# Experts' rows of blocks 13 to 16 added to the residual block by block, the read-back and the per-layer projection moved

## The chip, the core and the metric

The kernel runs on one core of a Trainium2 chip. TensorE (PE) multiplies, with its weight loads shown apart (PEld); VectorE (DVE), ScalarE (ACT) and GpSimd (POOL) do the elementwise work; SyncE (SP) issues the DMAs of the weights. The metric is the device time of one execution in microseconds, the median of several runs. One further execution was taken with the hardware profiler, and all rows below are from it.

## What is computed

Two models' layers run one after the other on 512 tokens of width 1024; everything is float32. The change touches the end of the second block: a mixture of experts (32 experts in four groups, one group and two experts of it for each token) and, behind it, a gated per-layer term.

```
y = 0
for grp in range(4):
    hid = silu(hf @ w_gate[e]) * (hf @ w_up[e])        # experts of width 256
    y = y + (hid * combine) @ w_down[e]                # two experts for each token
x = x + y
ple = rms_norm(p @ w_ple, ple_norm_g)
x = x + sigmoid(rms_norm(x, ple_gate_norm_g) @ w_ple_gate) * ple
```

## The kernel before

The residual is kept on the chip as eight tiles `h[k]` of 128 columns of the width by 512 tokens. The experts run in 17 blocks (NPOS) of 128 rows, two experts of 64 rows each; block 16 holds rows that didn't fit, and its experts' numbers are read from a register. For a block, the rows are gathered from DRAM (`xd`) by an indirect DMA on POOL's queue, turned by eight transposes on TensorE (`turn_rows`), multiplied with gate and up weights in two halves (`up_products`, `expert_up`), turned (`expert_turn`) and multiplied with the down weights (`expert_down`). The loop in `experts` lets block i's up products run with block i-1's turn and down products.

The weights come through `Ring`: 102 loads of 1 MB, four `w_eg` and two `w_ed` for a block, all issued by SP in the order in which they are used. A buffer is refilled with the next load when its matmuls are done (`release`, `fill`). There are 15 buffers that are refilled (eight `rawa`, three `rawb`, three `raw`, one `rawc`) and four pairs that serve once. `ring.gone` names the buffers that are no longer refilled (`rawb` and `rawc`, from block 8 on), `ring.hold` takes the next released buffers out for other uses (three at block 9, for `w_ple` and the projection's result; four at block 16). So eight buffers are left from block 9 on.

The results of blocks 0 to 13 (below NST = 14) are scattered to `yd` in DRAM by an indirect DMA on POOL's queue, each token's two rows to two places. Those of blocks 14 to 16 stay on the chip, split into a high and a low part (`pair_rows`), with a matrix of ones and zeros that spreads rows to tokens (`spread`). At block 16 four ring buffers are taken and `yd` is read back into them, four DMAs of 1 MB. Behind the last block and a branch (`overflow`, not taken here), `combine` multiplies the three blocks' parts by their spreads into eight PSUM banks (48 matmuls), adds the two halves of each read-back tile on VectorE and adds them to the same banks by 32 products with the identity. `per_layer` then adds the banks to the residual one by one, splits it (`ph`, `pl`), multiplies with `w_pg` in three-term products, and gates.

The projection `p @ w_ple` (`ple_steps`, 48 matmuls) runs in the middle of blocks 12 and 13 (PLE = 11). Its norm's row factors are formed in `per_layer`, where POOL multiplies the eight tiles by them.

All instructions of an engine run in the order in which the scheduler put them; a DMA that waits for its buffer holds up the DMAs behind it in SP's order. The lines that the steps name:

```
ring.gone = [self.merged] + [b for b in self.early if any(b[0] is x for x in self.spare)]   # 1691, block PLE - 3
ring.hold += 3                                                                              # 1693, block PLE - 2
ring.hold += TT                                                                             # 1707, block NPOS - 1
nc.sync.dma_start(y[tt], yd.rearrange("(a t p) d -> t p a d", a=2, t=TT)[tt])               # 1722
```

Of the kernel before, what the change touches and what calls it, by code (L numbers as in the profile page):

```python
# [22 lines left out]
P = 128  # L23
T = 512
# [28 lines left out]
NEX = 2 * (1 + OB)  # L53
NST = 14

# [334 lines left out]
class Kernel:  # L390
# [5 lines left out]
    ROWS = 7  # L396
    PLE = 11
    F0 = 6
# [1234 lines left out]
    def experts(self, rp, halves, *logits):  # L1633
# [4 lines left out]
        with ExitStack() as ctx:  # L1638
# [7 lines left out]
            tp = turns.enter_context(self.pool("eturn", side="right"))  # L1646
            xe, hid, turned, pairs, begun = {}, {}, {}, [], []
            gath = [tp.tile([P, D], F32, name=f"gath{i}") for i in range(2)]
# [23 lines left out]
            with ExitStack() as c2:  # L1672
# [5 lines left out]
                def turn():  # L1678
                    turned[i - 1] = self.expert_turn(tp, hid.pop(i - 1))
                    if between is not None:  # L1680
                        run(between)
                fetch(2)
                ple = own = None
                for i in range(NPOS + 1):
                    if i == 2:
                        next(routing)
                    if i == 5:
                        r["blocks"] = nc.values_load(r["over"][0:1, 0:1], min_val=0, max_val=NEX - 1,
                                                     skip_runtime_bounds_check_because=self.WHY)
                    if i == self.PLE - 3:  # L1690
                        ring.gone = [self.merged] + [b for b in self.early if any(b[0] is x for x in self.spare)]
# [12 lines left out]
                    if i == self.PLE + 1:  # L1704
                        next(ple)
                    if i == NPOS - 1:
                        ring.hold += TT
                    if i < NPOS:
                        between = rows(i + 1) if 0 < i < NPOS - 1 else None
                        act = self.expert_up(begun if i == 0 else self.up_products(xe.pop(i), ring), table[:, :, i], turn if i else None)  # L1710
                        if 0 < i < NPOS - 2:
                            fetch(i + 2)
                    else:
                        between = None
                        turn()
                    if i in (self.PLE + 1, self.PLE + 2):
                        next(ple)
                    if i == NPOS - 1:
                        y, taken = [], [ring.take() for _ in range(TT)]
                        for tt in range(TT):  # L1720
                            y.append(taken[tt].rearrange("p (a d) -> p a d", a=2))
                            nc.sync.dma_start(y[tt], yd.rearrange("(a t p) d -> t p a d", a=2, t=TT)[tt])
                    if i > 0:
                        acc = [self.bank() for _ in range(2)]
                        self.expert_down(turned.pop(i - 1), acc, ring)
                        if i - 1 >= NST:
                            ys = [late.tile([P, D], FR, name=f"ys{n}{i - 1}") if i < NPOS else tp.tile([P, D], FR, name=f"ys{n}", tag=f"xe{n}")
                                  for n in range(2)]
# [10 lines left out]
                downed = self.downed  # L1739
                self.overflow(tp, r)  # L1740
                sums = self.combine(pairs, y, downed)
            turns.close()
        return sums, ple, taken[0]

# [13 lines left out]

    def combine(self, pairs, y, downed):

        nc = self.nc
        o = [self.bank() for _ in range(KD)]
        for k in range(KD):
            for i, ((hi, lo), spread) in enumerate(pairs):
                for x in (hi, lo):
                    nc.tensor.matmul(o[k], x[:, P * k:P * k + P], spread, start=i == 0 and x is hi, stop=False)  # L1766
        for tt in range(TT):
            z = y[tt][:, 0]
            with self.tc.issue_after(downed.ins):
                nc.vector.tensor_tensor(z, z, y[tt][:, 1], op=ALU.add)  # L1770
            for k in range(KD):
                nc.tensor.matmul(o[k][:, P * tt:P * tt + P], z[:, P * k:P * k + P], self.ident, start=False, stop=tt == TT - 1)  # L1772
        return o

# [278 lines left out]
    def expert_up(self, steps, scales, between=None):  # L2053
# [6 lines left out]
        self.hidden = self.act(a, o[:, 0:256], AF.Silu, scale=scales[:, 0:1])  # L2060
        nc.vector.scalar_tensor_tensor(a, a, scales[:, 1:2], o[:, 256:512], op0=ALU.mult, op1=ALU.mult)
        return a
# [68 lines left out]
    def ple_steps(self, halves, late, room):  # L2131
# [16 lines left out]
        for m in range(KD):  # L2148
# [15 lines left out]
            if m % 4 == 3:  # L2164
                yield

    def per_layer(self, sums, ple, room):

        nc, W = self.nc, self.W
        with ExitStack() as ctx:  # L2170
# [14 lines left out]
            def gated(m, rb, o, ts):  # L2185
# [3 lines left out]
                nc.vector.scalar_tensor_tensor(x, x, 1.0, y, op0=ALU.add, op1=ALU.mult)  # L2189
                nc.vector.scalar_tensor_tensor(x, x, 0.5, self.h[m][:, ts], op0=ALU.mult, op1=ALU.add)  # L2190
# [16 lines left out]
            ps = self.bank()  # L2207
            for i, x in enumerate((self.ssq, self.ple_ssq)):
                for tt in range(TT):
                    nc.tensor.matmul(ps[:, TT * i + tt:TT * i + tt + 1], x[:, tt * P:tt * P + P], self.ones[:, 0:1], start=True, stop=True)  # L2210
            r = self.stat.tile([P, 2 * TT], F32, name="rcols", tag="rcol2")
            nc.vector.tensor_scalar(r, ps[:, :2 * TT], 1.0 / D, EPS, ALU.mult, ALU.add)
            nc.vector.reciprocal(r, r)
            self.act(r, r, AF.Sqrt)
            rows = []
            for i in range(2):
                product(3 + i)
                rows.append(self.to_rows(r[:, TT * i:TT * i + TT], ("rbc", "ssq")[i]))
            for x in self.ple:
                nc.gpsimd.tensor_tensor(x, x, rows[1], op=ALU.mult)  # L2220
            for m in range(KD - 1):
                if m > 4:
                    product(m)
                gated(m, rows[0], bank[m], slice(0, T))
            hi, lo = W.next("w_pg")
            for hf in range(2):
                ts = slice(256 * hf, 256 * hf + 256)
                o = self.bank()[:, 0:256]
                self.mm3(o, [((hi[:, P * k:P * k + P], lo[:, P * k:P * k + P]), (xs[k][0][:, ts], xs[k][1][:, ts])) for k in range(KD)])
                gated(KD - 1, rows[0], o, ts)  # L2230

# [14 lines left out]
```

## Time and profile before

| | us |
|---|---|
| median of three runs (2161.9, 2162.22, 2170.76) | 2162.22 |
| profiled execution, its own time | 2171.21 |
| span of the profile, first to last instruction | 2169.5 |
| TensorE busy | 2093.6 |
| VectorE busy | 1065.2 |
| ScalarE busy | 790.3 |
| POOL busy | 303.4 |

TensorE is busy in 97% of the span, but a busy TensorE includes matmuls that overlap and are modelled, and the share is a mean over stages with different limits. The share of the DMA engines, slice by slice, is low through most of the kernel and near full from about 1844 us on, where the experts' weights are streamed. The experts run from about 1828 to 2084 us, and from there to 2169.5 us come the combining, the gate's products and the output.

### The profile page before, as it was taken

To read this page: it belongs to the slowest core of one execution; us is meant where nothing else is said; L and a number is where in the kernel's file an instruction comes from. 1 tells how busy PE (TensorE), PEld (TensorE's weight loads), DVE (VectorE), ACT (ScalarE), POOL (GpSimd) and SP (SyncE) were. 2 spreads that over 40 slices of the span, in tenths; PEclk is the share of its full clock that TensorE was granted. 3 is DMA by queue.
4 is the path that set the end of the run, shared out by engine and by line. 5 is a ranking of instruction groups with operands and counts; after the bars stand their busy time and mean duration, and the time that the engine had idled before them with its cause. 6 is when DMAs were issued, how large, how long until landed. Compare 5 with 4: busy or idle time off the path is not lost. (4 is left out here: it accounts for less than half of the span.)

```text
span 2169.5 us, 25893 instructions
## 1 busy us (share of the span) xinstructions
PE 2093.6 (97%) x10282; PEld 1629.8 (75%) x10282; DVE 1065.2 (49%) x1928; ACT 790.3 (36%) x1189; POOL 303.4 (14%) x394
## 2 busy tenths in 40 slices
PE   8999999999999999999999999999999996998987
PEld 6678788888889878888788888888888884333456
DVE  7888644344467563554544344435654433112146
ACT  5676432223357443333433223342453221111223
POOL 3312200000013021221200000020110111111203
PEclk9899999999999999999999999999999998999999
DMA  5123332222224310101022222232211285999961
GB/s 188 59 79 109 150 111 98 99 88 95 88 72 147 115 35 15 40 24 55 21 96 97 90 95 97 88 136 78 79 58 67 96 323 198 374 420 416 380 278 39
DMA packets 71251, 281.72 MB, mean 130 GB/s; under 512 B 8859, under 2 KB 14235, under 8 KB 58452
## 3 DMA queue, kind: packets, MB, share of 16 engines
q1 hardware_dynamic: 60388, 264.63, 33.2%
q0 software_dynamic: 5504, 12.30, 1.5%
q10 hardware_dynamic: 5232, 3.07, 0.5%
q8 instruction: 83, 1.36, 0.2%
q14 instruction: 44, 0.36, 0.1%
HBM read 272.40 MB, written 15.73 MB: 133 GB/s over the span
## 5 line engine op out<-in xcount | busy, mean ns | idle before, releaser
L274 ACT ACTIVATE whi<-raw 128x1024 fp32r<-128x1024 f32 (+2 forms) x249 | 261.9, 1054 | 629.8 <-PE bank L421 578.6
L421 PE MATMUL bank<-xh,whi 128*128 128x512 f32 x1160 | 462.4, 399 | 8.6 <-ACT xh L431 7.8
L421 PE MATMUL bank<-xh,wlo 128*128 128x512 f32 x1160 | 456.4, 394 | 0.0
L421 PE MATMUL bank<-xl,whi 128*128 128x512 f32 x1160 | 453.1, 391 | 0.0
L275 DVE TENSOR_TENSOR wlo<-raw,whi 128x1024 fp32r<-128x1024 f32 (+2 forms) x249 | 314.8, 1268 | 213.9 <-ACT whi L274 210.0
L421 PEld LDWEIGHTS bank<-xh,whi 128*128 128x128 f32 x1160 | 219.3, 189 | 54.9 <-ACT xh L431 7.8
L421 PEld LDWEIGHTS bank<-xh,wlo 128*128 128x128 f32 x1160 | 218.4, 188 | 50.7 <-DVE wlo L275 0.3
L421 PEld LDWEIGHTS bank<-xl,whi 128*128 128x128 f32 x1160 | 219.0, 189 | 49.6 <-issue 1.2
L448 POOL TENSOR_TENSOR ssq<-ssq,sq 128x512 f32<-128x512 f32 x27 | 40.2, 1489 | 793.2 <-ACT sq L435 793.2
L421 PE MATMUL bank<-hidh,whi 128*128 128x512 f32 x352 | 137.0, 389 | 0.0
L421 PE MATMUL bank<-hidh,wlo 128*128 128x512 f32 x352 | 137.0, 389 | 0.0
L421 PE MATMUL bank<-hidl,whi 128*128 128x512 f32 x352 | 136.9, 389 | 0.0
L2049 PE MATMUL bank<-rawa,xe 128*64 128x512 f32 x328 | 93.8, 628 | 9.9 <-DMA rawa<-w_eg 6.3
L435 ACT ACTIVATE prob<-bank 128x512 f32<-128x512 f32 (+1 forms) x96 | 57.2, 596 | 110.8 <-PE bank L1238 81.3
L822 DVE TENSOR_TENSOR fb<-bank,rows 128x512 f32<-128x512 f32 x44 | 30.4, 690 | 133.5 <-PE bank L421 133.5
L1221 PEld LDWEIGHTS acc<-v,prob 128*128 128x128 f32 x640 | 79.8, 192 | 6.2 <-POOL prob L1248 2.3
L1221 PE MATMUL acc<-v,prob 128*128 128x96 f32 x640 | 82.2, 274 | 1.4 <-POOL prob L1248 1.4
L421 PEld LDWEIGHTS bank<-hidh,wlo 128*128 128x128 f32 x352 | 66.1, 188 | 13.9
L421 PEld LDWEIGHTS bank<-hidl,whi 128*128 128x128 f32 x352 | 66.1, 188 | 13.8
L421 PEld LDWEIGHTS bank<-hidh,whi 128*128 128x128 f32 x352 | 66.1, 188 | 13.6
L819 DVE TENSOR_TENSOR fa<-bank,rows 128x512 f32<-128x512 f32 x44 | 30.4, 690 | 88.2 <-PE bank L421 88.2
L2049 PEld LDWEIGHTS bank<-rawa,xe 128*64 128x64 f32 x328 | 27.4, 144 | 59.2 <-issue 48.5
(562 smaller groups left out, 3696.2 us busy)
## 6 DMA issues: line engine op xcount, KB each, us to landing
raw<-w_gu SPq DMA_DIRECT2D x44, 1024.0 KB, 4.8
rawa<-w_eg SPq DMA_DIRECT2D x41, 1024.0 KB, 14.1
raw<-w_dn SPq DMA_DIRECT2D x20, 1024.0 KB, 4.8
raw<-w_eg SPq DMA_DIRECT2D x16, 1024.0 KB, 13.7
rawa<-w_ed SPq DMA_DIRECT2D x16, 1024.0 KB, 14.9
raw<-w_mix SPq DMA_DIRECT2D x12, 1024.0 KB, 4.9
raw<-w_ed SPq DMA_DIRECT2D x10, 1024.0 KB, 15.7
rawb<-w_eg SPq DMA_DIRECT2D x7, 1024.0 KB, 17.1
```

The source lines that it names most:

```text
L274: nc.scalar.activation(hi, r, AF.Copy)
L275: nc.vector.tensor_tensor(lo, r, hi.bitcast(F32), op=ALU.subtract)
L421: i = nc.tensor.matmul(o, a, b, start=first and n == 0, stop=last and n == N - 1)
L435: return self.nc.scalar.activation(o, i, f, **kw)
L448: self.nc.gpsimd.tensor_tensor(self.ssq, self.ssq, sq, op=ALU.add)
L819: nc.vector.tensor_tensor(a, og, rbc, op=ALU.mult)
L822: nc.vector.tensor_tensor(b, ov, rbc, op=ALU.mult)
L1221: i = nc.tensor.matmul(a[:, h * AW:h * AW + AW], e[:K, h * P:h * P + P], v, start=first and h == 0, stop=last and h == HPG - 1)
L2049: last = nc.tensor.matmul(o[s], xe[:, 4 * pi + k, s], w(k), start=pi == 0 and k == 0, stop=pi == 1 and k == 3)
```

## The change

NST goes from 14 to 13, so block 13 stays on the chip too. The parts of blocks 13, 14 and 15 are no longer kept for `combine`: `add_block` multiplies one block's part by its spread, bank by bank, and VectorE adds each bank to `h[k]` at once, in the middle of the next block (or behind `expert_down` for block 15). Only block 16 is left to `combine`, 16 matmuls. The read-back is taken at the end of block 14, into buffers held from block 13 on; `add_rows` adds its halves on POOL, transposes the tiles on TensorE and adds the banks to `h[k]`, within block 16. `ring.gone` is set at block 0. PLE goes from 11 to 6: the projection runs in blocks 7 and 8, three buffers are held at block 4, and the norm's factors and POOL's eight multiplications follow in block 9. In `per_layer` the row statistics of the projection and POOL's multiplications are gone, and the factor 0.5 has moved into the norm's factors.

```diff
-NST = 14
+NST = 13
-    PLE = 11
+    PLE = 6
...
+                    while adds:
+                        run(adds.pop(0))
...
-                    if i == self.PLE - 3:
+                    if i == 0:
                         ring.gone = [self.merged] + [b for b in self.early if any(b[0] is x for x in self.spare)]
...
+                    if i == NST:
+                        ring.hold += TT
                     if i == NPOS - 1:
-                        ring.hold += TT
+                        adds.append(self.add_rows(y))
...
-                    if i in (self.PLE + 1, self.PLE + 2):
+                    if i in (self.PLE + 1, self.PLE + 2, self.PLE + 3):
                         next(ple)
-                    if i == NPOS - 1:
-                        y, taken = [], [ring.take() for _ in range(TT)]
-                        for tt in range(TT):
-                            y.append(taken[tt].rearrange("p (a d) -> p a d", a=2))
-                            nc.sync.dma_start(y[tt], yd.rearrange("(a t p) d -> t p a d", a=2, t=TT)[tt])
...
-                            pairs.append((self.pair_rows(*ys, acc), self.spread(late.tile([P, T], FR, name=f"spread{i - 1}"), r, i - 1)))
+                            ys = [late.tile([P, D], FR, name=f"ys{n}", bufs=2) for n in range(2)]
+                            part = self.pair_rows(*ys, acc), self.spread(late.tile([P, T], FR, name="spread", bufs=2), r, i - 1)
+                            if i < NPOS:
+                                adds.append(self.add_block(*part))
...
+                    if i == NST + 1:
+
+                        y = [ring.take() for _ in range(TT)]
+                        for tt in range(TT):
+                            nc.sync.dma_start(y[tt].rearrange("p (a d) -> p a d", a=2), yd.rearrange("(a t p) d -> t p a d", a=2, t=TT)[tt])
...
+    def block_sum(self, part, spread, k):
+
+        o = self.bank()
+        for x in part:
+            self.nc.tensor.matmul(o, x[:, P * k:P * k + P], spread, start=x is part[0], stop=x is part[1])
+        return o
+
+    def add_block(self, part, spread):
+        for k in range(KD):
+            o = self.block_sum(part, spread, k)
+            self.nc.vector.tensor_tensor(self.h[k], self.h[k], o, op=ALU.add)
+            yield
+
+    def add_rows(self, y):
+
+        for x in y:
+            self.nc.gpsimd.tensor_tensor(x[:, :D], x[:, :D], x[:, D:], op=ALU.add)
+        for k in range(KD):
+            o = self.bank()
+            for tt, x in enumerate(y):
+                self.nc.tensor.transpose(o[:, P * tt:P * tt + P], x[:, P * k:P * k + P], self.ident)
+            self.nc.vector.tensor_tensor(self.h[k], self.h[k], o, op=ALU.add)
+            yield
+
+    def combine(self, part, spread):
+        return [self.block_sum(part, spread, k) for k in range(KD)]
...
+        r = self.rms_cols(ssq, tag="rcol2")
+        nc.vector.tensor_scalar(r, r, 0.5, None, ALU.mult)
+        rows = self.to_rows(r)
+        for x in self.ple:
+            nc.gpsimd.tensor_tensor(x, x, rows, op=ALU.mult)
+        yield
...
-            for x in self.ple:
-                nc.gpsimd.tensor_tensor(x, x, rows[1], op=ALU.mult)
```

How the change moves instructions is shown at three places. The first is SP's order in the first blocks, the refills of the ring behind block 1's and 2's matmuls (a row is the issuing line, the buffer, the source and the shape). Before:

```order
L343 DMA rawa7_13935<-w_ed 128x2048
L343 DMA rawb0_13925<-w_ed 128x2048
L343 DMA rawb1_13926<-w_eg 128x2048
L343 DMA rawb2_13927<-w_eg 128x2048
L343 DMA raw_14211<-w_eg 128x2048
L343 DMA raw_14212<-w_eg 128x2048
L343 DMA raw_14213<-w_ed 128x2048
L343 DMA rawc_14325<-w_ed 128x2048
L343 DMA rawa0_13928<-w_eg 128x2048
```

and now:

```order
L343 DMA rawa7_13935<-w_ed 128x2048
L343 DMA raw_14211<-w_ed 128x2048
L343 DMA raw_14212<-w_eg 128x2048
L343 DMA raw_14213<-w_eg 128x2048
L343 DMA rawa0_13928<-w_eg 128x2048
L343 DMA rawa1_13929<-w_eg 128x2048
L343 DMA rawa2_13930<-w_ed 128x2048
L252 DMA rawa3_13931<-w_ple 128x2x1024
L343 DMA rawa6_13934<-w_ed 128x2048
```

The refills of `rawb` and `rawc` are gone, and the load of `w_ple` into `rawa3` stands here.

The second is SP's order at the last expert weights. Before, the loads of `w_ed` for blocks 15 and 16 (the rows ISA set the address of an expert read from a register), the first two reads of `yd`, and the branch:

```order
L343 DMA rawa6_13934<-w_ed 128x2048
L343 DMA rawa7_13935<-w_ed 128x2048
L343 ISA
L343 DMA raw_14211<-w_ed 128x2048
L343 ISA
L343 DMA raw_14212<-w_ed 128x2048
L1722 DMA raw_14213<-yd_104 128x2x1024
L1722 DMA rawa0_13928<-yd_104 128x2x1024
L1688 TENSOR_LOAD over_14346
L2109 COMPARE_AND_BRANCH
```

and now, from the four `w_eg` of block 15 on (the two `w_ed` are block 14's, the register load belongs to block 16):

```order
L343 DMA rawa2_13930<-w_eg 128x2048
L343 DMA rawa6_13934<-w_eg 128x2048
L343 DMA rawa7_13935<-w_eg 128x2048
L343 DMA raw_14211<-w_eg 128x2048
L1744 DMA raw_14212<-yd_104 128x2x1024
L1744 DMA raw_14213<-yd_104 128x2x1024
L1744 DMA rawa0_13928<-yd_104 128x2x1024
L1744 DMA rawa1_13929<-yd_104 128x2x1024
L343 DMA rawa2_13930<-w_ed 128x2048
L343 DMA rawa6_13934<-w_ed 128x2048
L612 TENSOR_LOAD over_14346
L343 ISA
```

The four reads of `yd` have moved from behind the last `w_ed` to a place ahead of the last ten expert weights: two `w_ed` of block 14, and then the four `w_eg` of block 16, two `w_ed` of block 15 and two of block 16, which follow.

The third is VectorE's order behind the branch, the start of the tail. Before, three of the four adds of read-back halves, splits of `w_pg` (`wlo`), and the first residual tile:

```order
L2109 UNCONDITIONAL_BRANCH
L1770 TENSOR_TENSOR rawa0_13928<-rawa0_13928 128x1024
L1770 TENSOR_TENSOR rawa1_13929<-rawa1_13929 128x1024
L1770 TENSOR_TENSOR rawa2_13930<-rawa2_13930 128x1024
L275 TENSOR_TENSOR wlo_16655<-rawa6_13934,whi_16654 128x1024
L275 TENSOR_TENSOR wlo_16659<-rawa6_13934,whi_16658 128x1024
L2196 TENSOR_TENSOR h0_76<-h0_76,bank_16554 128x512
L275 TENSOR_TENSOR wlo_16663<-rawa7_13935,whi_16662 128x1024
L275 TENSOR_TENSOR wlo_16667<-rawa7_13935,whi_16666 128x1024
L432 SCALAR_TENSOR_TENSOR pl0_16680<-h0_76,vecs_86,ph0_16679 128x512
L2196 TENSOR_TENSOR h1_77<-h1_77,bank_16555 128x512
```

and now:

```order
L2126 UNCONDITIONAL_BRANCH
L2219 TENSOR_TENSOR h0_76<-h0_76,bank_16734 128x512
L275 TENSOR_TENSOR wlo_16767<-rawa7_13935,whi_16766 128x1024
L275 TENSOR_TENSOR wlo_16771<-rawa7_13935,whi_16770 128x1024
L275 TENSOR_TENSOR wlo_16775<-raw_14211,whi_16774 128x1024
L275 TENSOR_TENSOR wlo_16779<-raw_14211,whi_16778 128x1024
L432 SCALAR_TENSOR_TENSOR pl0_16792<-h0_76,vecs_86,ph0_16791 128x512
L2219 TENSOR_TENSOR h1_77<-h1_77,bank_16737 128x512
```

The adds of read-back halves are gone from here, and four splits of `w_pg` instead of two stand between the first add to the residual and its low part `pl0`.

On TensorE, the 16 matmuls of `add_block` stand in the first half of the next block (ten ahead of the rest of that half, six behind it) for blocks 13 and 14, and behind `expert_down` of block 15 for that block. The 32 transposes of `add_rows` stand ahead of block 16's second half.

## Rows read from the trace of the kernel before

**Rows 1.** Busy time by stretch: PE, PEld, DVE, ACT, POOL, clock, DMA share, GB/s

```profile
1860.00:2000.00 140.00, 129.56 (x611) 49.66 (x610) 24.63 (x50) 24.12 (x46) 20.51 (x21) 1.00 1.01 416
2020.00:2040.00 20.00, 20.00 (x85) 8.95 (x85) 1.78 (x4) 6.76 (x12) 7.13 (x6) 1.00 0.92 351
2040.00:2080.00 40.00, 36.50 (x158) 12.45 (x158) 5.70 (x10) 5.78 (x12) 1.00 (x1) 1.00 1.01 410
```

**Rows 2.** Timeline, VectorE, the gated products that end blocks 6, 7, 12, 13

```profile
1917.84 0.48 DVE L2061 SCALAR_TENSOR_TENSOR eact<-eact,etable,bank 128x256 f32<-128x256 f32 x1 [3.28 <-ACT eact L435]
...
1929.53 0.48 DVE L2061 SCALAR_TENSOR_TENSOR eact<-eact,etable,bank 128x256 f32<-128x256 f32 x1 [3.27 <-ACT eact L435]
...
2013.30 0.48 DVE L2061 SCALAR_TENSOR_TENSOR eact<-eact,etable,bank 128x256 f32<-128x256 f32 x1 [12.37 <-ACT eact L435]
...
2033.29 0.48 DVE L2061 SCALAR_TENSOR_TENSOR eact<-eact,etable,bank 128x256 f32<-128x256 f32 x1 [12.38 <-ACT eact L435]
```

**Rows 3.** Timeline of TensorE around the last block and the combining matmuls

```profile
2065.38 0.64 PE L2049 MATMUL bank<-rawa,xe 128*64 128x512 f32 x1 [0.95 <-DMA rawa<-w_eg]
...
2070.34 3.22 PE L2049 MATMUL bank<-rawa,xe 128*64 128x512 f32 x13 [1.30 <-DMA rawa<-w_eg]
...
2079.62 4.36 PE L2082 MATMUL bank<-raw,eh 128*64 128x512 f32 x16 [0.53 <-ACT eh L435]
2086.67 12.88 PE L1766 MATMUL bank<-spread,ys 128*128 128x512 f32 x48 [2.70 <-DVEq L2109]
```

**Rows 4.** Timeline of all engines in the tail (start, length, engine, line, operation)

```profile
2105.17 0.69 DVE L2196 TENSOR_TENSOR h<-h,bank 128x512 f32<-128x512 f32 x1 [4.81 <-PE bank L1772]
2105.78 2.35 DVE L275 TENSOR_TENSOR wlo<-rawa,whi 128x1024 fp32r<-128x1024 f32 x2
2108.05 0.74 DVE L432 SCALAR_TENSOR_TENSOR pl<-h,vecs,ph 128x512 fp32r<-128x512 f32 x1
...
2128.01 1.03 PE L2210 MATMUL bank<-ones,plessq 128*128 128x1 f32 x8
...
2142.64 12.77 POOL L2220 TENSOR_TENSOR rawa<-rawa,rows 128x512 f32<-128x512 f32 x8 [17.37 <-ACT rows L435]
...
2158.23 0.28 PE L421 MATMUL bank<-ph,wlo 128*128 128x256 f32 x1
...
2164.91 0.42 DVE L2187 TENSOR_TENSOR raw<-bank,rows 128x256 f32<-128x256 f32 x1
```

**Rows 5.** DMA queues from 1700 to 2100 us: packets, MB, share of time

```profile
q1 hardware_dynamic: 18827, 120.72, 75.3%
q0 software_dynamic: 4464, 8.11, 5.6%
```

**Rows 6.** Timeline of SP: refills of the ring in blocks 0 to 4

```profile
1835.57 0.33 SPq L343 DMA_DIRECT2D rawa<-w_eg  x1
...
1860.61 5.39 SPq L343 DMA_DIRECT2D rawb<-w_eg  x2
1866.10 4.73 SPq L343 DMA_DIRECT2D raw<-w_eg  x2
...
1873.93 0.33 SPq L343 DMA_DIRECT2D rawc<-w_ed  x1
...
1894.31 0.38 SPq L343 DMA_DIRECT2D rawa<-w_eg  x1
```

**Rows 7.** Timeline of SP: the read-back's issues

```profile
2068.22 0.38 SPq L1722 DMA_DIRECT2D raw<-yd  x1
2069.06 17.39 SPq L1722 DMA_DIRECT2D rawa<-yd  x3
```

**Rows 8.** Timeline of TensorE behind the routing's gather, block 0

```profile
1828.06 1.94 PE L2035 MATMUL bank<-ident,gath 128*128 128x128 f32 x8 [6.00 <-DMA gath<-xd,gidx]
1829.93 5.61 PE L2049 MATMUL bank<-rawa,xe 128*64 128x512 f32 x16
...
1837.28 1.07 PE L2035 MATMUL bank<-ident,gath 128*128 128x128 f32 x8
```

More of the change, by code (lines that the diff above doesn't have):

```diff
@@ L1646, in experts @@
             tp = turns.enter_context(self.pool("eturn", side="right"))
-            xe, hid, turned, pairs, begun = {}, {}, {}, [], []
+            xe, hid, turned, begun, adds = {}, {}, {}, [], []
             gath = [tp.tile([P, D], F32, name=f"gath{i}") for i in range(2)]
@@ L1714, in experts @@
                         between = None
+                        while adds:
+                            run(adds.pop(0))
                         turn()
-                    if i in (self.PLE + 1, self.PLE + 2):
+                    if i in (self.PLE + 1, self.PLE + 2, self.PLE + 3):
                         next(ple)
-                    if i == NPOS - 1:
-                        y, taken = [], [ring.take() for _ in range(TT)]
-                        for tt in range(TT):
-                            y.append(taken[tt].rearrange("p (a d) -> p a d", a=2))
-                            nc.sync.dma_start(y[tt], yd.rearrange("(a t p) d -> t p a d", a=2, t=TT)[tt])
                     if i > 0:
@@ L1737, in experts @@
                         hid[i] = act
+                    if i == NST + 1:
+                        y = [ring.take() for _ in range(TT)]
+                        for tt in range(TT):
+                            nc.sync.dma_start(y[tt].rearrange("p (a d) -> p a d", a=2), yd.rearrange("(a t p) d -> t p a d", a=2, t=TT)[tt])
                 assert W.ld == len(W.order)
-                downed = self.downed
                 self.overflow(tp, r)
-                sums = self.combine(pairs, y, downed)
+                sums = self.combine(*part)
             turns.close()
-        return sums, ple, taken[0]
+        return sums, y[0]
     def spread(self, out, r, blk):
@@ L1757, in pair_rows @@
         return hi, lo
-    def combine(self, pairs, y, downed):
-        nc = self.nc
-        o = [self.bank() for _ in range(KD)]
-        for k in range(KD):
[L1764 to L1773, printed above, removed]
+    def block_sum(self, part, spread, k):
[4 more added lines that the diff above has]
+    def add_block(self, part, spread):
+        for k in range(KD):
+            o = self.block_sum(part, spread, k)
[12 more added lines that the diff above has]
+        return [self.block_sum(part, spread, k) for k in range(KD)]
     def router(self, kp, steps):
@@ L2060, in expert_up @@
         self.hidden = self.act(a, o[:, 0:256], AF.Silu, scale=scales[:, 0:1])
[L2061 removed]
+        self.scaled = nc.vector.scalar_tensor_tensor(a, a, scales[:, 1:2], o[:, 256:512], op0=ALU.mult, op1=ALU.mult)
         return a
@@ L2165, in ple_steps, with per_layer @@
                 yield
-    def per_layer(self, sums, ple, room):
+        r = self.rms_cols(ssq, tag="rcol2")
[4 more added lines that the diff above has]
+        yield
+    def per_layer(self, sums, room):
         nc, W = self.nc, self.W
@@ L2189, in gated @@
                 nc.vector.scalar_tensor_tensor(x, x, 1.0, y, op0=ALU.add, op1=ALU.mult)
-                nc.vector.scalar_tensor_tensor(x, x, 0.5, self.h[m][:, ts], op0=ALU.mult, op1=ALU.add)
+                nc.vector.tensor_tensor(x, x, self.h[m][:, ts], op=ALU.add)
                 nc.sync.dma_start(self.out[m * P:m * P + P, ts], x)
@@ L2206, in per_layer @@
                         terms(m, early[m], k - lag, k - lag + 1)
[L2207 to L2218, printed above, removed]
-            for x in self.ple:
-                nc.gpsimd.tensor_tensor(x, x, rows[1], op=ALU.mult)
+            r = self.rms_cols(self.ssq, tag="rcol2")
+            product(3)
+            rows = self.to_rows(r)
+            product(4)
             for m in range(KD - 1):
@@ L2223, in per_layer @@
                     product(m)
-                gated(m, rows[0], bank[m], slice(0, T))
+                gated(m, rows, bank[m], slice(0, T))
             hi, lo = W.next("w_pg")
@@ L2229, in per_layer @@
                 self.mm3(o, [((hi[:, P * k:P * k + P], lo[:, P * k:P * k + P]), (xs[k][0][:, ts], xs[k][1][:, ts])) for k in range(KD)])
-                gated(KD - 1, rows[0], o, ts)
+                gated(KD - 1, rows, o, ts)
 def kernel(**inputs):
```

2 lines of the change are left out of this document (removed).

## The prediction

> **What bounds the kernel now.** I read the busy time by stretches first. From 1860 to 2080 us, where most of the 17 expert blocks run, the DMA share is 1.01 at 410 to 416 GB/s, except around 2020 to 2040 (0.92) [rows 1]. The reader should see that TensorE is also busy there, and ask which of the two ends the waits. The block ends say it: blocks 6 and 7 are 11.7 us apart, as long as their matmuls take, while the two blocks that also carry the per-layer projection end 20.0 us apart [rows 2]. In the last two blocks the matmuls wait for weights again (0.95 and 1.30 us), and the two pairs of loads of block 16 arrive 4.96 us apart [rows 3]. So the DMA queue bounds the end of the experts, and what counts is how many megabytes stand ahead of the last w_ed, and whether the queue ever runs empty.
>
> Behind the experts stands a tail in which the queue no longer counts. The last expert matmul ends at 2083.98, 48 matmuls of `combine` take 12.88 us [rows 3], 32 products with the identity follow, and the first add to the residual starts only at 2105.17. The last matmul of all starts at 2158.23, the span ends at 2169.5, 11.1 us after it: VectorE is late, because eight multiplications on POOL (12.77 us) run until 2155.4 and it needs their results [rows 4].
>
> **Unit prices.** The SP queue moved 120.72 MB in 75.3% of 400 us [rows 5]: 115 loads of 1 MB in 301 us, 2.62 us each in a full queue. The 31 gathers and scatters of rows (17 and 14 by the loops) took 5.6% of the same stretch, 0.72 us each. Six loads, a gather and a scatter per block make 17.2 us of queue against 11.7 us of matmuls. Half an `expert_up`, or an `expert_down`, is 3.2 to 3.5 us [rows 3].
>
> **Fewer buffers from the start.** The order of SP shows that rawb and rawc are no longer refilled after their first use and that three rawa are held at block 4 (they were at block 9). Before, 23 refills were issued from 1835.57 to the one at 1894.31, three rawb, three raw and one rawc among them [rows 6]. Now it is 16, w_ple included, the last of them behind the same block's matmuls, by the order of SP. Blocks 0 to 4 run on loads that came earlier, so TensorE's pace doesn't change, and the queue has 16 x 2.62 + 6 x 0.72 = 46 us of work in 59 us: empty for 13 us. Before it was empty for 1.6 us in the projection's stretch (0.92 of 20 us) [rows 1]; moved to blocks 7 and 8 the projection finds a queue that lags, so that gap goes. Net +11.5 us (bounds 0, if the queue weren't the bound later, to 13). The projection itself costs as much TensorE time at blocks 7 and 8 and is covered by the queue. Its eight POOL multiplications, 12.8 us at block 9, stand ahead of the scatter of block 8 and the gather for block 13, which is used in block 12; I price them at nothing, the cover being the 5.5 us by which the queue exceeds the matmuls in each of blocks 10 to 12. One scatter less: -0.7 us.
>
> **The read-back ahead of ten loads.** The change's words put it behind all weights; SP's order doesn't. The four reads of `yd` stand behind block 15's w_eg and ahead of w_ed of 14, w_eg of 16, w_ed of 15 and w_ed of 16. Before, they were the last but for w_pg: two issued at 2068 to 2069, the others behind the branch [rows 7]. In a full queue they cost 4 x 2.62 = 10.5 us, waited for by `expert_down` of block 14, with all of TensorE's order behind it.
>
> **Four buffers and more matmuls.** From block 13 on four buffers are left, two pairs A and B that take turns. Let X be the landing of block 15's last w_eg. Before: six loads (15.7 us) and a half block (3.5): block 16's second half ends at X + 19.2, measured 2073.98, so X is 2054.8. Now: read-back X + 10.5, w_ed of 14 at X + 15.7, down(14) ends X + 19.3 and frees A for the second w_eg pair of 16. The first pair lands at X + 20.9, TensorE goes on with a matmul, a turn (0.4), ten matmuls of block 14's rows at 12.88 / 48 = 0.27 (2.7), the rest of the half (3.0): X + 27.0; six more (1.6): X + 28.6; `add_rows`. Its 32 transposes are 4.3 us by the gather's eight in 1.07 [rows 8] or 5.5 us if VectorE's eight adds at 0.69 [rows 4] pace them; the order has them wait for VectorE's banks, so 5.0. POOL's four adds of 1024 columns, 2.6 to 3.3 us each by the eight of 512 in 12.77 [rows 4], end by X + 16, under the wait. Second half: X + 37.1. Against X + 19.2 that is 17.9 us, 10.5 of them the read-back and 7.4 the rest (bounds 3, all additions hidden under the wait, to 14, none of them).
>
> From there to the last expert matmul it was 10.0 us [rows 3]; now down(15) 3.5, sixteen matmuls of block 15's rows 4.3, turn and eviction 1.1, down(16) 3.6: 12.5 us, +2.5. TensorE will stand still about 8 us ahead of down(14). After the 6.00 us wait in the routing, eight transposes took 1.94 instead of 1.07 and 16 matmuls 5.61 instead of 3.22 to 3.65 us [rows 8]: down(14) loses some 2.5 us, of which 1.2 get past the landing at X + 20.9. [...]
>
> Last expert matmul: 11.5 - 0.7 + 17.9 + 2.5 + 1.2 = 32.4 us later.
>
> **The tail.** Before, from the start of `combine` (C, 2086.67) to the end: 82.8 us. Now 16 matmuls instead of 48 and 32 products. The first residual add starts at C + 1 instead of C + 18.5; behind it stand four w_pg splits at 1.2 us instead of two (rows 4 has two in 2.35), since the loads come only now, so the first `pl` ends at C + 7.1 instead of C + 22.1: 15.0 us won. Eight small matmuls of row statistics less: 1.0 us (a row's 1.03). With POOL's multiplications gone, VectorE keeps up and the end follows the last matmul by 4.9 instead of 11.1 us (4.6 from the last gate's start at 2164.91 to the end, 0.3 for the matmul's own end) [rows 4]: 6.2 us. Together 22.2 us (18 to 27).
>
> **Sum.** +32.4 - 22.2 = +10.2 us. The profiled execution's own time is 2171.21 us, 9 us above the median of the runs (2162.22); I add to the median: 2172.4 us, +0.47%.
>
> **Rivals.** *The queue has slack.* If the matmuls, not the queue, set the pace in blocks 10 to 14, neither the empty 13 us nor the read-back costs anything; of the added 13.6 us of matmuls ahead of block 16's second half 7.5 hide under its former waits, +6.1 + 2.5 - 22.2 = -13.6 us: 2148.6. It decides where the DMA share in these blocks falls under 1. For it: the 0.92 of the projection's stretch; against it: 17.2 us of queue against 11.7, and 1.01 on either side of it [rows 1].
>
> *Only one of the two delays reaches the end.* The early gap is made up, or the read-back runs behind the weights after all as the words say: one term of 10.5 to 11.5 goes, about -1 us: 2161. For it: blocks 7 and 8 take 20 us for 17.2 us of queue. Against it: an empty queue's time isn't made up unless it would have been empty later too.
>
> [...]
>
> **How the numbers follow.** Forecast 0.54 (2164 to 2180), one delay only 0.19, clock 0.15, slack 0.12. A measurement here can tell some 0.5% (10.8 us: 2151.4 to 2173.0) from no change. Faster by more: the slack case, 0.12. Within: the one-delay case and half the forecast, 0.47. Slower by more: the rest, 0.41. The range from 2154 to 2185 leaves out the slack case and the far end of the clock's.
>
> **What would show it.** In the profile after: DMA share under 1 between 1865 and 1900; reads of yd issued ahead of ten weight loads; a wait of about 8 us of down(14) for w_ed; last expert matmul near 2116; `combine` to end near 60 us. The forecast is wrong if that matmul ends before 2106, or if the share falls under 1 in blocks 10 to 14.

## The result

The changed kernel takes 2175.36 us, median of 12 runs, against 2163.76 us for the kernel before in the same series; the ratio of the runs is 1.0051, with a 95% interval from 1.0039 to 1.0063. It is slower by half a per cent, 11.0 us by that ratio. The medians are 11.6 us apart, and one run of the kernel before, at 3477.43 us, is far off all others. The forecast was 2172.4 us and +10.2 us, so sign and size held. The terms behind it held less well: two errors of some 5 us each, which ran against each other, lie among them, and the experiments below say which.

### The profile page after: what moved, and what is told of

It is laid out like the page before. It is cut to its first block, busy times and chain, and to the rows that moved or that the text cites. A ratio compares the mean times of both kernels' runs of the same rounds, so it can differ in the third digit from the quotient of the medians.

```text
span 2170.0 us, 25913 instructions
## 1 busy us (share of the span) xinstructions
PE 2089.4 (96%) x10266; PEld 1626.3 (75%) x10266; DVE 1075.3 (50%) x1965; ACT 792.9 (37%) x1192; POOL 308.6 (14%) x397
## 5 line engine op out<-in xcount | busy, mean ns | idle before, releaser
L2066 PE MATMUL bank<-rawa,xe 128*64 128x512 f32 x352 | 106.1, 617 | 10.8 <-DMA rawa<-w_eg 7.1
## 6 DMA issues: line engine op xcount, KB each, us to landing
rawa<-w_ed SPq DMA_DIRECT2D x21, 1024.0 KB, 10.6
```

The source lines that it names most:

```text
L2066: last = nc.tensor.matmul(o[s], xe[:, 4 * pi + k, s], w(k), start=pi == 0 and k == 0, stop=pi == 1 and k == 3)
```

## The profile after

The profiled execution of the changed kernel took 2171.69 us with a span of 2170.0 us, only 0.5 us more than that of the kernel before. The two can't be laid on each other as they are, because the execution of before lost time ahead of all that was changed. Two rows of TensorE show where: the 16 matmuls of block 1's first half (start, length, engine, line, operation, the idle time before). Before:

```profile
1845.59 6.31 PE L2049 MATMUL bank<-rawa,xe 128*64 128x512 f32 x16 [3.65 <-issue]
```

and after:

```profile
1840.50 3.65 PE L2066 MATMUL bank<-rawa,xe 128*64 128x512 f32 x16 [3.66 <-issue]
```

The same matmuls behind the same wait took 6.31 us in one execution (granted clock 0.57) and 3.65 in the other (1.00). With 5.1 us from stages ahead of it, the execution of before ends block 2 at 1871.06, that after at 1863.30. So all comparisons below start at block 2's end, read from VectorE's gated product that ends a block, and go in two pieces: to the gated product of block 16 (the last up products), and from there to the span's end. Before, these rows are

```profile
1871.06 0.48 DVE L2061 SCALAR_TENSOR_TENSOR eact<-eact,etable,bank 128x256 f32<-128x256 f32 x1 [3.28 <-ACT eact L435]
...
2074.53 0.48 DVE L2061 SCALAR_TENSOR_TENSOR eact<-eact,etable,bank 128x256 f32<-128x256 f32 x1 [9.11 <-ACT eact L435]
```

and after

```profile
1863.30 0.48 DVE L2078 SCALAR_TENSOR_TENSOR eact<-eact,etable,bank 128x256 f32<-128x256 f32 x1 [2.40 <-ACT eact L435]
...
2092.83 0.48 DVE L2078 SCALAR_TENSOR_TENSOR eact<-eact,etable,bank 128x256 f32<-128x256 f32 x1 [1.11 <-ACT eact L435]
```

That is 203.47 us before and 229.53 us after, 26.1 us more for the experts. From block 16's product to the end of the span (2169.5 and 2170.0) it is 94.97 and 77.17 us, 17.8 us less. The sum is +8.3 us, a little under the 11.0 us of the runs.

**The early queue**, as [rows 1] show it for later stretches: the 60 us that begin 27.3 us ahead of block 2's end (busy time of PE, PEld, DVE, ACT, POOL, then the granted clock, the DMA share and GB/s). Before and after:

```profile
1843.80:1903.80 60.00, 58.21 (x284) 23.24 (x286) 11.05 (x25) 8.60 (x17) 9.09 (x9) 0.94 0.93 378
```

```profile
1836.00:1896.00 60.00, 56.34 (x288) 22.55 (x286) 17.74 (x46) 10.96 (x20) 9.53 (x9) 1.00 0.86 330
```

At 416 GB/s the queue would move 25.0 MB here. After, it moved 19.8 and so was 12.4 us short. Before, it moved 22.7 and was already 5.5 us short. The difference is 6.9 us, but the two clocks differ (0.94 and 1.00): with its slow matmuls inside, the stretch of before starts 2.7 us of work later. Two of the kernels below have the same clock here, e9, which refills as before, and e11, which refills as after:

```profile
1836.85:1896.85 60.00, 57.20 (x284) 23.07 (x286) 12.07 (x27) 8.60 (x17) 9.09 (x9) 0.97 0.95 383
```

```profile
1838.47:1898.47 60.00, 57.20 (x284) 23.02 (x286) 16.09 (x37) 10.38 (x19) 9.57 (x9) 0.97 0.84 319
```

They are 4.8 and 14.0 us short of full, so at the same clock the change opens 9.2 us. The hole of before lies ahead of where [rows 1] begin:

```profile
1840.00:1860.00 20.00, 16.35 (x68) 5.62 (x64) 7.76 (x27) 1.93 (x4) 0.99 (x1) 0.83 0.77 304
```

**The read-back and the last blocks.** SP's issues behind block 15's w_eg, which answer to [rows 7]:

```profile
2049.65 1.02 SPq L1744 DMA_DIRECT2D raw<-yd  x2
2050.71 1.40 SPq L1744 DMA_DIRECT2D rawa<-yd  x2
2055.64 1.19 SPq L343 DMA_DIRECT2D rawa<-w_ed  x2
```

and when the four reads landed, told by POOL's adds that wait for them:

```profile
2060.87 2.34 POOL L1781 TENSOR_TENSOR raw<-raw 128x1024 f32<-128x1024 f32 x1 [26.27 <-DMA raw<-yd]
2063.44 2.34 POOL L1781 TENSOR_TENSOR raw<-raw 128x1024 f32<-128x1024 f32 x1 [0.23 <-DMA raw<-yd]
2065.99 2.34 POOL L1781 TENSOR_TENSOR rawa<-rawa 128x1024 f32<-128x1024 f32 x1 [0.21 <-DMA rawa<-yd]
2068.49 2.34 POOL L1781 TENSOR_TENSOR rawa<-rawa 128x1024 f32<-128x1024 f32 x1 [0.16 <-DMA rawa<-yd]
```

They land 2.5 to 2.6 us apart, 10.2 us for four, one after the other in a full queue, and only then comes w_ed. On TensorE, where [rows 3] stood before:

```profile
2070.97 5.51 PE L2099 MATMUL bank<-rawa,eh 128*64 128x512 f32 x14 [8.48 <-DMA rawa<-w_ed]
...
2085.01 0.38 PE L1785 MATMUL bank<-ident,raw 128*128 128x128 f32 x2
...
2088.59 3.65 PE L2066 MATMUL bank<-rawa,xe 128*64 128x512 f32 x16
...
2100.35 3.65 PE L2099 MATMUL bank<-rawa,eh 128*64 128x512 f32 x16 [0.53 <-ACT eh L435]
2106.80 5.51 PE L1769 MATMUL bank<-spread,ys 128*128 128x512 f32 x16 [2.79 <-PEq L2126]
```

The first row is the wait that was forecast, 8.48 us of `expert_down` of block 14 for w_ed, and behind it matmuls at a mean granted clock of 0.72: 14 in 5.51 us, where 16 take 3.65 in the fourth row. The transposes of `add_rows` begin at 2085.01 and block 16's second half follows at 2088.59, without a wait. The last row is `combine`.

**The tail**, ScalarE and TensorE behind `combine`, where [rows 4] stood before:

```profile
2110.41 2.00 ACT L274 ACTIVATE whi<-rawa 128x1024 fp32r<-128x1024 f32 x2 [5.73 <-SPq L2126]
2112.32 1.98 ACT L274 ACTIVATE whi<-raw 128x1024 fp32r<-128x1024 f32 x2
2114.21 0.71 ACT L431 ACTIVATE ph<-h,vecs 128x512 fp32r<-128x512 f32 x1
2114.97 0.78 PE L421 MATMUL bank<-ph,whi 128*128 128x512 f32 x1 [2.66 <-ACT ph L431]
2116.85 0.80 PE L421 MATMUL bank<-pl,whi 128*128 128x512 f32 x1 [1.10 <-DVE pl L432]
```

The first matmul that needs the first `pl` starts 10.05 us after `combine` (2106.80). In the trace of before it was 2108.85 against 2086.67, 22.18 us: a gain of 12.1 us.

## The experiments

Ratios are to runs of the kernel before on the same chip; 0.01% is 0.22 us. The kernels are compared through these ratios, and by their intervals a difference of two is uncertain by some 3 to 4 us. The last two columns are the pieces named above, in us, each from one profile.

| kernel | median us | ratio, 95% interval | block 2 to 16 | to the end |
|---|---|---|---|---|
| before | 2163.76 | 1 | 203.47 | 94.97 |
| after | 2175.36 | 1.0051 [1.0039, 1.0063] | 229.53 | 77.17 |
| e1 quarter of the read-back | 2168.28 | 1.0012 [1.0001, 1.0023] | 222.78 | 77.40 |
| e2 refills end at block 3 | 2168.10 | 1.0017 [1.0005, 1.0029] | 224.26 | 76.92 |
| e3 projection's part only | 2163.10 | 0.9994 [0.9984, 1.0004] | 211.04 | 85.04 |
| e4 adds' part only | 2182.50 | 1.0082 [1.0066, 1.0098] | 226.93 | 84.27 |
| e5 e3, refills end at 3 | 2158.39 | 0.9963 [0.9950, 0.9975] | 205.47 | 85.12 |
| e6 hold a block later | 2172.89 | 1.0037 [1.0026, 1.0048] | 228.03 | 76.32 |
| e7 read-back behind weights | 2164.82 | 0.9995 [0.9983, 1.0006] | 213.80 | 84.21 |
| e9 norm and POOL only | 2157.25 | 0.9968 [0.9954, 0.9982] | 204.56 | 84.39 |
| e10 e7 without early gap | 2165.25 | 1.0000 [0.9987, 1.0012] | 210.78 | 85.64 |
| e11 e7 on four buffers | 2171.87 | 1.0028 [1.0017, 1.0040] | 216.03 | 87.70 |

**e1, the read-back cut to a quarter.**

```diff
-    nc.sync.dma_start(y[tt].rearrange("p (a d) -> p a d", a=2), yd.rearrange("(a t p) d -> t p a d", a=2, t=TT)[tt])
+    nc.sync.dma_start(y[tt].rearrange("p (a d) -> p a d", a=2)[:, :, 0:256],
+                      yd.rearrange("(a t p) d -> t p a d", a=2, t=TT)[tt][:, :, 0:256])
```

> The changed kernel, but each of the four reads of yd moves a quarter of its columns (1 MB in all instead of 4; this leaves three quarters of the scattered rows out of the sum). Theory: the read-back stands in a full queue ahead of ten weight loads and is paid in full, so 3 MB less at 2.62 us each bring the wait of 8.48 us of down(14) to under 1 us, down(14) runs at 3.6 us instead of 5.5, and the end comes 8 to 10 us earlier, near 2166. Rival: the ping-pong of four buffers sets the pace there anyway and the wait only moves to the weights of block 16: under 3 us earlier, 2172 or more.

It came 0.39% under the changed kernel, 8.4 us, as the theory said for 7.9 us of queue and the clock. From block 14's gated product to block 16's, the stretch with the reads, the profiles give 48.28 us for the changed kernel and 39.78 for e1, 8.5 us; the table's column shows less, since this execution of e1 had lost 1.8 us between block 2 and block 14. The wait of 8.48 us is down to this, and there are four matmuls in 1.90 us behind it, at full pace:

```profile
2072.27 1.90 PE L2099 MATMUL bank<-rawa,eh 128*64 128x512 f32 x4 [1.23 <-DMA rawa<-w_ed]
```

So within the scatter of the runs the read-back is paid for in full: nothing ahead of the end covers it.

**e2, the refills go on until block 3.**

```diff
-                    if i == 0:
+                    if i == 3:
                         ring.gone = [self.merged] + [b for b in self.early if any(b[0] is x for x in self.spare)]
```

> The changed kernel, but rawb and rawc are refilled until block 3 instead of block 0. In the trace of the changed kernel the queue is empty for 8.5 us in blocks 1 to 4 against 4.5 us before. Theory: the gap is smaller than predicted and each us of it is paid, so the end comes 3 to 5 us earlier, near 2171. Rival as predicted: the early gap costs 11.5 us, so 2164. Second rival: the lead is lost again when only four buffers are left, so nothing changes, 2175.

It came 0.34% under the changed kernel, 7.4 us, between the theory (3 to 5) and the prediction's 11.5. The share of busy engines had misled me when I set the theory: a share of 0.86 stood for 330 of 416 GB/s, 0.79. Over the same 60 us, at the clock of 0.97 that e11 had, e2 moves 367 GB/s where e11 moves 319. That is 2.9 MB or 6.9 us of queue, about what came back.

**e3, the projection's part alone on the kernel before.**

```diff
-    PLE = 11
+    PLE = 6
-                    if i == self.PLE - 3:
+                    if i == 0:
                         ring.gone = [self.merged] + [b for b in self.early if any(b[0] is x for x in self.spare)]
...
```

The norm's factors, POOL's multiplications and `per_layer` are as in the change; NST = 14, `combine` and the read-back as before.

> The kernel before with the projection's part alone: PLE 6, the early end of the refills, the norm's factors and POOL's multiplications in block 9, the shorter last stage. The 48 combining matmuls and the read-back at the end stay. Theory: early gap +2.5, last stage -7.2 (1.0 statistics, 6.2 VectorE no longer late): 2159, 5 us under the kernel before. Rival as predicted: +11.5 - 7.2, 2168.

No difference from before: 1.3 us faster, with an interval that holds no change, between the two expectations. The two columns say why: 7.6 us more to block 16, 9.9 less behind it. Both effects are there and cancel.

**e5, e3 with the refills until block 3.**

```diff
-                    if i == 0:
+                    if i == 3:
                         ring.gone = [self.merged] + [b for b in self.early if any(b[0] is x for x in self.spare)]
```

> e3 (the projection's part alone) with rawb and rawc refilled until block 3 instead of block 0. Theory: e3 gained 10 us behind its last expert matmul and lost 7.5 us ahead of it to the early gap, of which the later end of the refills gives 5 back, as it did in e2: 2158. Rival: the three buffers held at block 4 make the gap whatever is refilled, under 1.5 us from e3: 2162.

As the theory said: 2158, 0.31% or 6.7 us under e3, and by the profile 5.6 us of it ahead of block 16. It is faster than both kernels.

**e9, e3 with the projection back at blocks 12 and 13**: only the norm's factors and POOL's multiplications are early.

```diff
-    PLE = 6
+    PLE = 11
-                    if i == 0:
+                    if i == self.PLE - 3:
                         ring.gone = [self.merged] + [b for b in self.early if any(b[0] is x for x in self.spare)]
```

> e3 with the projection back at blocks 12 and 13 (PLE 11, refills until block 8): of the change only the norm's factors and POOL's eight multiplications are early, now in block 14. Theory: the 10 us behind the last expert matmul stay, and the early gap is not there: 2154 to 2156, the fastest. Rival: POOL's 10 to 13 us in block 14 hold up the scatters and gathers of the last blocks: as before, 2163.

0.32% or 6.9 us faster than before, near the forecast and not apart from e5. Its gain behind block 16 is 10.6 us, 1.5 of which `combine` won by a better clock (11.38 us at 1.00 against 12.88 at 0.87), and it pays 1.1 us ahead of it. POOL's multiplications stand in block 14 and cost no more than that. e9 and e3 differ in the refills, in the buffers held from block 4 on and in the place of the projection: 0.26%, 5.6 us by the runs, 6.5 by the profiles. That this is the early gap, e5 says, which changes the refills alone and gets 6.7 us back.

**e4, the adds' part alone**, with PLE 11 and the refills until block 8 as before.

```diff
-    PLE = 6
+    PLE = 11
-                    if i == 0:
+                    if i == self.PLE - 3:
                         ring.gone = [self.merged] + [b for b in self.early if any(b[0] is x for x in self.spare)]
...
```

`ple_steps` and `per_layer` are as before the change; NST = 13, `add_block`, `add_rows` and the early read-back as changed.

> The changed kernel with the projection, its norm and POOL's multiplications as before (PLE 11, refills until block 8): the adds by blocks, the earlier read-back and the four buffers alone. Theory: the two parts add up, so this one is the changed kernel's +11 less e3's -5, +13 to +16: near 2178. Rival: at blocks 12 and 13 the projection's 8 us of matmuls each cover the queue's gap of 5 us that the four buffers leave, +6 to +9: near 2171.

It is 0.82% or 17.8 us slower than before, more than either theory gave. Together with e3 that is 16.5 us, not the 11.0 of the whole change, so the parts don't seem independent, though the intervals together allow nearly as much. The stretch in which e4 has the projection and only four buffers:

```profile
2020.00:2040.00 20.00, 19.70 (x81) 8.47 (x79) 1.77 (x3) 6.75 (x12) 6.11 (x5) 1.00 0.44 166
```

The queue is busy for 0.44 of 20 us and moves 166 GB/s, where it was 0.92 and 351 in the same work before [rows 1]: with four buffers, too few come free while TensorE does the projection. The move to blocks 7 and 8 spares the changed kernel that.

**e6, the four buffers held from block 14 on.**

```diff
-                    if i == NST:
+                    if i == NST + 1:
                         ring.hold += TT
```

> The changed kernel with the four buffers for the read-back held from block 14 on instead of block 13. Theory: the queue stood empty for 5 us between 2024 and 2036 because four buffers can't hold a block's six loads; with eight buffers for a block longer that gap goes, the end comes 3 to 5 us earlier: 2171. Rival: the reads of yd now wait at SP for the buffers of block 14 and hold up the ten weight loads behind them, so nothing is gained or it is slower: 2175 to 2180.

3.0 us faster than the changed kernel (0.14%), at the low end of the theory, but their intervals overlap. In the changed kernel the stretch from 2020 to 2040 reads

```profile
2020.00:2040.00 20.00, 15.91 (x68) 5.48 (x64) 1.77 (x3) 1.94 (x4) 1.40 (x2) 1.00 0.76 296
```

and in e6 this and the next one read

```profile
2020.00:2040.00 20.00, 15.79 (x72) 5.67 (x70) 1.77 (x3) 1.94 (x4) 1.51 (x2) 1.00 1.01 416
2040.00:2060.00 20.00, 19.51 (x86) 8.44 (x84) 9.55 (x15) 1.94 (x4) 2.35 (x1) 1.00 0.72 290
```

So the gap in the queue, 5.8 us by bytes in the changed kernel and 6.1 in e6, moves one block on with the hold and stays. It belongs to running on four buffers. TensorE has no use for it: in the changed kernel it waits for weights three times there,

```profile
2023.90 3.22 PE L2066 MATMUL bank<-rawa,xe 128*64 128x512 f32 x13 [1.78 <-DMA rawa<-w_eg]
...
2029.03 2.79 PE L2099 MATMUL bank<-rawa,eh 128*64 128x512 f32 x10 [0.50 <-DMA rawa<-w_ed]
...
2040.36 3.22 PE L2066 MATMUL bank<-rawa,xe 128*64 128x512 f32 x13 [2.11 <-DMA rawa<-w_eg]
```

so both sides are idle in the same stretch: by the program a buffer is refilled only when its matmuls are done.

**e7, the read-back behind all weights.**

```diff
-                    if i == NST:
-                        ring.hold += TT
                     if i == NPOS - 1:
-                        adds.append(self.add_rows(y))
+                        ring.hold += TT
...
+                    if i == NPOS - 1:
+                        y, taken = [], [ring.take() for _ in range(TT)]
...
```

The reads and the 32 products with the identity in `combine` are as before, the latter behind block 16's part alone.

> The changed kernel with the read-back where it was before (buffers held and read at the last block, behind all expert weights) and brought in by 32 products with the identity behind the 16 combining matmuls; the adds of blocks 13 to 15 and the projection as changed. Theory: the read-back's 10.5 us and the four buffers' 5 us go, the tail loses 7 us of its gain: 8 us earlier, 2167. Rival: the read-back isn't what the end waits for, 2175 to 2182.

0.56% or 12.1 us under the changed kernel, more than expected, and level with before and with e3. 15.7 us come back ahead of block 16, 7.0 are given up behind it. Against e3, which adds nothing on the way, it gains 0.8 us behind block 16 and loses 2.8 ahead of it: on top of e3, adding the blocks' rows on the way is worth nothing.

**e11, e7 with the four buffers held from block 13 on.**

```diff
-                    if i == NPOS - 1:
+                    if i == NST:
                         ring.hold += TT
```

> e7 (read-back behind all weights) with the four buffers for it held from block 13 on, as in the changed kernel: the last four blocks run on four buffers, but no read stands ahead of their weights. Between the ends of block 16's up products the changed kernel is 15.7 us behind e7. Theory: 10 of them are the read-back, 5 to 6 the four buffers, so here the last block ends 5 to 6 us later than in e7, 2169. Rival: four buffers alone give most of the 15.7 us, 2174 or more. Second rival: nothing, 2165, and all of it is the read-back.

0.33% or 7.1 us slower than e7, a little over the 5 to 6 expected; of the 5.7 us that the profiles show, 2.2 lie ahead of block 16's product and 3.5 between it and the start of `combine`, around the last `expert_down`. The changed kernel is another 0.23% or 5.0 us slower: in the profiles 13.5 us more ahead of block 16 (10.2 of queue; the transposes take 3.6 and the slow matmuls lose 2.3, in part under it), less the 10.5 us that it then spares the tail.

**e10, e7 with the projection back at blocks 12 and 13.**

```diff
-    PLE = 6
+    PLE = 11
-                    if i == 0:
+                    if i == self.PLE - 3:
                         ring.gone = [self.merged] + [b for b in self.early if any(b[0] is x for x in self.spare)]
```

> e7 with the projection back at blocks 12 and 13 (PLE 11, refills until block 8): e9 plus the adds by blocks, the read-back behind all weights. Theory: e7 against e3 shows that adding blocks 13 to 15 on the way gains nothing once the read-back is out of the way, since the matmuls taken out of the last stage are paid in the last blocks; as e9, 2157. Rival: with eight buffers and no early gap the last blocks have room for them and 4 to 5 us of the combining matmuls are saved: 2152.

Both expectations were wrong. It is level with before, 0.32% or 6.9 us slower than e9, from which it differs in the adds alone. In e9 only 2.4 us of waits for weights are left in the last blocks to hide matmuls under:

```profile
2059.07 0.64 PE L2049 MATMUL bank<-rawa,xe 128*64 128x512 f32 x1 [0.65 <-DMA rawa<-w_eg]
...
2064.52 3.22 PE L2049 MATMUL bank<-rawa,xe 128*64 128x512 f32 x13 [1.79 <-DMA rawa<-w_eg]
```

and e10 puts 32 matmuls of 0.26 us ahead of block 16's product (2077.66), for the rows of blocks 13 and 14. The last row but one is block 15's, behind it:

```profile
2049.20 2.55 PE L1768 MATMUL bank<-spread,ys 128*128 128x512 f32 x10
...
2055.25 1.66 PE L1768 MATMUL bank<-spread,ys 128*128 128x512 f32 x6
...
2065.77 2.56 PE L1768 MATMUL bank<-spread,ys 128*128 128x512 f32 x10
2071.84 1.66 PE L1768 MATMUL bank<-spread,ys 128*128 128x512 f32 x6
...
2080.50 3.98 PE L1768 MATMUL bank<-spread,ys 128*128 128x512 f32 x16
...
2092.33 2.00 PE L1795 MATMUL bank<-spread,ys 128*128 128x512 f32 x5 [3.45 <-DVE rawa L1799]
```

2 x 4.2 - 2.4 = 6.0 us, measured 6.2 to block 16. The shorter `combine` doesn't give it back: from block 16's product to the first matmul that needs `pl` it is 32.95 us, 32.79 in e9. Block 15's matmuls stand in between, the start of `combine` waits 3.45 us for VectorE's add of the read-back's halves (the last row; 2.69 in e9), and its 16 matmuls take 5.50 us. In e7 the early gap had made waits under which the matmuls could hide: e3, with the same gap and no adds, waits 6.8 us for weights in six places from 2039 us on, e7 only once there, 2.05 us.

## Why the prediction held, and where it didn't

A chain of kernels, each differing from the one ahead in one part, takes the 11.0 us apart by the runs, each step uncertain by 3 to 4 us: the norm and POOL early -6.9 (e9), the early gap +5.6 (e3), the adds on the way +0.2 (e7), four buffers +7.1 (e11), the read-back ahead, and brought in on the way, +5.0 (the changed kernel). The sizes belong to this order: on e9, without the early gap, the adds cost 6.9 us (e10), and once they are in, the early gap costs nothing (e7 is 1.1 us under e10).

**The early gap, 11.5 us forecast, 5.6 to 6.5 measured.** This is the step that failed. That the queue would stand empty for 13 us was right: it was 12.4 us short of full. That before it had been full but for 1.6 us was wrong: it was 5.5 us short in the same blocks. The stretch from 1840 to 1860, with its share of 0.77, stands just ahead of [rows 1]. I counted the new hole and not the old one; at one clock the net hole is 9.2 us (e9 and e11 above). And the gap of 1.6 us in the projection's stretch was read from the share of 0.92: by its 351 GB/s [rows 1] it is 3.1 us, and in e3 the queue is full there (418 GB/s). 9.2 less 3.1 is 6.1 us, between the 5.6 and the 6.5 measured. The bounds of this term, 0 to 13, held the value. (The 23 refills that I counted before are 22; no sum uses them.)

**The read-back, 10.5 us.** Right in place and size: issued ahead of ten loads, 10.2 us in the queue, waited for by `expert_down` of block 14 (8.48 us against 8 forecast), and 8.4 us come back when three quarters of it go (e1). That the change's words said otherwise was worth reading SP's order for: e7 is what the words describe. It lies 1.1 us under before, where the rival in which the read-back runs behind the weights had -1 us, but that agreement is luck: in e7 the four buffers' cost goes too (7.1 us, e11) and the tail loses 7.0 us, neither of which the rival had.

**Four buffers and matmuls, 7.4 us, and the clock, 1.2.** From e3 to the changed kernel the way to block 16 grows by 18.5 us, where the terms (17.9 with the read-back, 1.2, less the scatter's 0.7) give 18.4. Inside, the sizes are shifted. The 32 transposes took 3.6 us (2085.01 to 2088.59) instead of 5.0, and block 16's first weights weren't waited for. In their place a gap came that I had not priced, the queue 5.8 us short of full in blocks 13 and 14 for want of buffers, with TensorE waiting as well (e6). The agreement of this sum is partly luck.

**The clock.** Behind the wait of 8.48 us 14 matmuls took 5.51 us; 14 at the pace of 16 in 3.65 are 3.2, so 2.3 us were lost (2.5 forecast). The granted clock was 0.72 there. It did not go on through the last blocks: behind it, from 2077.40 to 2080.00, the clock was 1.00 and ten matmuls took 2.53 us. The chances count a case of the clock, 0.15, for a loss that does go on; the profile after doesn't show it. Slower matmuls came behind waits for weights of 8.48, 7.79 and 7.08 us (14 in 5.51 us in the changed kernel, 6.32 in e4, 7.00 in e6). Of the waits around 2 us most left 13 matmuls at 3.22 us (in the changed kernel after 2.11 us, clock 1.00), and a few did not: behind 1.96 us in the changed kernel they took 4.92 us, the clock being 0.65.

**The tail, -22.2 with +2.5 ahead of it forecast, -17.8 measured.** From block 16's product to `combine` it was 12.14 us and is 13.97: +1.8. From the first `pl` to the end it was 60.65 and is 53.15: -7.5, where the statistics and VectorE's lag were forecast at 7.2. From `combine` to the first `pl` the gain is 12.1 instead of 15.0 us. I had put VectorE's four splits of `w_pg` between the first add and `pl`, and had not looked at ScalarE: it waits 5.73 us for SP to get past the branch (three of the four loads of `w_pg` had been issued by 2104.03), then makes four `whi` of 1.0 us, and only then `ph`, on which `pl` waits. That is read from the trace; no run changes this order. `combine` itself ran at a mean granted clock of 0.69, 5.51 instead of 4.3 us, but the path to the first `pl` goes through ScalarE and doesn't see it.

**The sum.** The early gap was priced some 5 us too dear, and the tail was to win 2 us more than it did; the rest of what the profiles show (+8.3 against +10.2) is about 1 us, the other way. The runs say 11.0. That the whole came within 1 us of them is therefore in part luck; the sign rests on terms that the experiments bear out, the read-back above all.

**The signs.** The share under 1 early, the order of the reads, the wait of 8 us and `combine` to end (63.2 us, "near 60") came as written. The last expert matmul near 2116 ended at 2104.0, which by the letter of the last sentence (under 2106) speaks against the forecast. That mark was set in the time of an execution that had already lost 7.8 us by block 2. Counted from there it is 2111.8. A mark should have been given as a distance, not as a time. The other one, a share under 1 in blocks 10 to 14, did come, in blocks 13 and 14 alone (0.76), but TensorE waited for weights there too: a queue without buffers, and no slack.

## What to carry to other kernels

When a change takes buffers from a queue that sets the pace, price the new hole less the old one, in bytes moved over the same stretch of work in both. A transfer moved ahead of a full queue's weights cost its whole length here (10.2 us of queue; with 7.9 us of it gone 8.4 us came back, e1), and matmuls taken out of the last stage gained only as much as there were waits where they went (8.4 us of matmuls against 2.4 us of waits in e10, 6.2 us paid). Parts that each look good can undo one another: here the norm alone is worth 0.32%, and all of the change together costs 0.51%.

## What was not expected of the hardware

- With the same instructions up to there, the changed kernel and e1 end block 2 at 1863.30 and 1871.02 us. In the kernel before, 2.7 us of such a loss was TensorE's clock behind a wait of 3.65 us in block 1: 16 matmuls took 6.31 us at a granted clock of 0.57, and 3.65 us at 1.00 behind the same wait in the changed kernel.
- The share of busy DMA engines overstated what moved where the queue had gaps: over the same 60 us the shares of 0.93 and 0.86 are 4.2 us apart, the bytes 6.9 us.
- POOL's eight multiplications took 9.88 us in block 9, beside the experts, and 12.77 us at the end of the kernel before [rows 4].
